# A decoder layer on one core: the 16 gated-attention units as seven block products, made ahead of the attention

## The chip, the core and the metric

The kernel runs on one core of one Trainium2 chip. A core has five engines that each follow their own list of instructions in order and wait for each other by semaphores: TensorE (PE, matrix products; its weight loads are shown apart, as PEld), VectorE (DVE), ScalarE (ACT), GpSimd (POOL) and SyncE (SP). In this kernel nearly every transfer between memory and the core is issued by SyncE, one after the other. The metric is the device time of one launch in microseconds, the median of several runs.

## The reference

One layer of a decoder, all in float32, for 1024 tokens and a model width of 2048:

```python
h = rmsnorm(x, g_pre)                       # over the 2048 columns
u = h @ w_in                                # split into the groups below
gq, gk, gv, g_gate, g_lr, sq, sk, sv, s_gate = split(u)
log_a = log_sigmoid(g_lr @ w_a2 + b_a) / 16
o_gla = gla_chunked(gq, gk, gv, log_a)      # 4 heads: q and k of 128 columns, v of 256
o_gla = rmsnorm(o_gla, g_gla_head) * silu(g_gate)
o_sb  = stick_breaking(sq, sk, sv) * silu(s_gate)   # 8 heads of 128 columns
mix = concat(o_gla, o_sb) @ w_out
x = x + rmsnorm(mix, g_post)
x = x + sigmoid(x @ w_ple_gate + b) * (p @ w_ple_proj)
```

The gated linear attention (GLA) keeps a state that decays by `log_a`; the stick-breaking attention weights position s for query t by `sigmoid(z_ts)` times the product of `1 - sigmoid(z_tj)` over the positions between them.

## The kernel before

Activations lie transposed: 128 features on the partitions, tokens along the free axis, in two halves of 512 tokens (`hf`). `x` is 16 blocks of 128 features. The columns of `w_in` that the attention needs are cut into 40 units of 128 columns: 16 for GLA (k, q and two of v for each of four heads), 24 for stick-breaking (k, q, v for each of eight heads).

Every float32 operand is split into two rounded parts, a high `hi` (ACT copies) and a low `lo` (VectorE subtracts), and a product is three matmuls: hi x hi, lo x hi, hi x lo. `split` (L111 to L113) does this everywhere, for weights and activations.

`dense` (L143) makes one unit: for each of 16 feature blocks and both halves three matmuls of 128x128 by 128x512 into a PSUM tile `dn`, 96 in all. Four weight quarters of 256 KB are loaded by `wload`, each into one of two `raw` buffers, and split into one of four `hi` and `lo` buffers. The norm of x is not applied to x: a unit's result is multiplied by `rstd` when it leaves PSUM. The first two units are interleaved with the loading of x, and the low-rank gate (`lr_ps`) with them.

After every feature block `dense` calls `step`, which lets other work move on: one piece of the queue `urgent`, and `rate[1]` pieces of the queue `jobs`. Jobs are generators: `gla(h)` for each GLA head and `sb()` for all stick-breaking heads. Each `yield` ends a piece. Thus the attention is laid between the dense products, by default in the order of the program; the scheduler may then move instructions by priorities (`high_priority` lifts weight loads and the emptying of PSUM) and by its own estimate of when operands are there. What it leaves on each engine is fixed when the kernel is built.

A stick-breaking head has 12 scores (6 items of two). For each score (`scores`): three matmuls into a PSUM tile `z` (two buffers), two sigmoids on ACT (into a tile `kq` with the tag X, L588, and a tile `sg` with the tag E or E2, L589), on diagonal blocks three GpSimd instructions, a reversed product scan on VectorE (L599), a multiply (L604), and `turn_by_dma` (L327): ACT copies the result apart into 16-bit planes in another X tile (L329), and a DMA transposes it into an E tile. X and E have two buffers each. The transposed weights are put together (L614) and split 8 pieces later, and multiplied with V another 8 pieces later. V itself is turned in the same way, by `turn`, through one X and one E tile for each half.

Before the change each unit's result goes straight into an SBUF tile of the attention (`evac_plain`, or `evac_turned` for V), so a head starts when its units are made, and a stick-breaking head waits for its three.

The later stages (the gate columns of `w_in`, `w_out`, `w_ple_gate`) already work by seven block products: the operands are cut into two by two blocks, sums S1 to S4 of blocks are kept in memory, and seven products of half the width replace eight, by Winograd's form of Strassen's scheme. The sums of x for the gates are made by `x_sums` beside the units.

Of the kernel before, what the change touches and what calls it, by code (L numbers as in the profile page):

```python
# [18 lines left out]
P = 128  # L19
# [26 lines left out]
RATE_GLA = 1.0  # L46
W0, W1, W2 = 3, 6, 1
RATE_SB = 0.9
# [5 lines left out]
LAG = 10  # L54
RATE_BG = 0.5
RATE_TAIL = 1.1
LAST_11 = 4
PACE_QKV, PACE_TAIL = 15, 4
# [3 lines left out]
def layer(ctx, tc, xT, w_in, w_gate, w_lr, w_a2, b_a, g_pre, g_head, w_out, g_post,  # L62
# [101 lines left out]
    pace = [0, PACE_QKV]  # L164
# [39 lines left out]

    def U(n):
        return [w_in[n, q] for q in range(4)]


    x_act = {hf: [None] * KT for hf in HALVES}
    pair = {}  # L210
    acc = {}
    lr_ps = {0: ps("t"), 1: ps("o")}
    first = [{hf: ps("dn") for hf in HALVES} for _ in range(2)]
    with tc.tile_pool(name="start", bufs=1) as sp:
        ones = sp.tile([P, P], F32, name="ones")
# [5 lines left out]
        lr_raw = sp.tile([P, KT, 16], F32, name="lr_raw")  # L221
        lr_w = sp.tile([P, KT, 32], F32, name="lr_w")
# [4 lines left out]
        raws = {hf: [] for hf in HALVES}  # L227
        squares_left = deque()

        def square(hf, k, raw):  # L230
            if k == 0:
                acc[hf] = new_rstd(hf)
                A.activation(acc[hf], raw, AF.Square)
                return
            sq = sp.tile([P, HT], F32, tag=f"sq{hf}", name=nm("sq"), bufs=2)
            A.activation(sq, raw, AF.Square)
            (V if hf == 0 else G).tensor_tensor(acc[hf], sq, acc[hf], op=ALU.add)

        for q in range(4):
            w = [wload(w_in[n, q]) for n in range(2)]  # L240
            for kk in range(4):
                k = 4 * q + kk
                sl = slice(kk * P, (kk + 1) * P)
                for hf in HALVES:
                    raw = sp.tile([P, HT], F32, tag="xraw", name=nm("xraw"), bufs=20)
                    dma(raw, part(xT[hf, k // 2], k))
                    raws[hf].append(raw)
                    if k % 2 == 0:
                        pair[hf] = act_wide(hf, k // 2)
                    ah, al = (part(t, k) for t in pair[hf])  # L250
                    x_act[hf][k] = (ah, al)
                    A.activation(ah, raw, AF.Copy, scale=gpre_s[:, k:k + 1])  # L252
# [15 lines left out]
        while squares_left:  # L268
            square(*squares_left.popleft())
# [475 lines left out]

# [613 lines left out]
```

## Time and profile before

| | us |
|---|---|
| median of 3 runs | 2095.12 (2091.56 to 2095.52) |
| the profiled execution | 2091.95 |
| its span, first to last instruction | 2089.9 |
| PE busy | 2068.4 (99%) |
| DVE busy | 1487.0 (71%) |
| ACT busy | 875.6 (42%) |
| POOL busy | 106.5 (5%) |

The profile names an instruction by its line, its engine, its operation and its tiles (out<-in, buffer numbers left out). Many instructions bear a helper's line: L101 is every matmul, L112 and L113 the two halves of every split. A wait row says which engine and line waited for which, the total in us, how often, and the longest. A window row gives a stretch of the span and its length, and then the busy time of PE, PEld, DVE, ACT and POOL, each with the number of instructions, the granted TensorE clock, the share of the DMA engines and GB/s. Matmuls overlap: the mean duration of one is longer than the time from one start to the next.

### The profile page before, as it was taken

To read this page: it belongs to the slowest core of one execution; us is meant where nothing else is said; L and a number is where in the kernel's file an instruction comes from. 1 tells how busy PE (TensorE), PEld (TensorE's weight loads), DVE (VectorE), ACT (ScalarE), POOL (GpSimd) and SP (SyncE) were. 2 spreads that over 40 slices of the span, in tenths; PEclk is the share of its full clock that TensorE was granted. 3 is DMA by queue.
4 is the path that set the end of the run, shared out by engine and by line. 5 is a ranking of instruction groups with operands and counts; after the bars stand their busy time and mean duration, and the time that the engine had idled before them with its cause. 6 is when DMAs were issued, how large, how long until landed. Compare 5 with 4: busy or idle time off the path is not lost.

```text
span 2089.9 us, 26754 instructions
## 1 busy us (share of the span) xinstructions
PE 2068.4 (99%) x9712; PEld 1708.3 (82%) x9712; DVE 1487.0 (71%) x2243; ACT 875.6 (42%) x1390; POOL 106.5 (5%) x228
## 2 busy tenths in 40 slices
PE   9999999999999999999999999999999999999998
PEld 6788888888888888888888788888888888787887
DVE  8657777676767667666567667788777787876665
ACT  7433333343455455555456413344233434323332
POOL 3100000000011011101001000000000000000000
PEclk9999999999999999999999999999999999999999
DMA  6222222222244344433336687888877586876663
GB/s 217 69 69 74 85 74 85 67 85 67 72 113 105 93 99 121 107 100 97 78 84 152 211 307 282 317 316 289 329 288 261 182 322 216 304 266 213 226 199 113
DMA packets 229812, 352.81 MB, mean 169 GB/s; under 512 B 124464, under 2 KB 129456, under 8 KB 229680
## 3 DMA queue, kind: packets, MB, share of 16 engines
q1 hardware_dynamic: 229104, 349.01, 52.1%
q10 hardware_dynamic: 576, 2.10, 0.3%
q8 instruction: 76, 1.25, 0.3%
q14 instruction: 56, 0.46, 0.1%
HBM read 249.85 MB, written 73.92 MB: 155 GB/s over the span
## 4 chain that ended last, share of the span: by engine, by line
PE 50%; DVE 9%; DMA 8%; issue 2%; ACT 2%; POOL 0%; SPq 0%; DVEq 0%; ACTq 0%; POOLq 0%
PE dn L101 45%; DMA wr<-w_g 3%; PE z L101 2%; PE t L101 2%; DVE wl L113 2%; DMA E<-X 2%; DMA wr<-w_out 1%; PE o L101 1%; DVE wr L872 1%; DVE al L113 1%; DMA ar<-og_d 1%; DVE ar L869 1%; DVE X L599 1%; DVE wr L869 1%; DVE ev L869 0%
## 5 line engine op out<-in xcount | busy, mean ns | idle before, releaser
L101 PE MATMUL dn<-ah,hi 128*128 128x512 f32 x1408 | 563.2, 400 | 1.5 <-ACT hi L112 1.3
L101 PE MATMUL dn<-al,hi 128*128 128x512 f32 x1408 | 551.0, 391 | 0.2 <-DVE al L253 0.2
L101 PE MATMUL dn<-ah,lo 128*128 128x512 f32 x1408 | 550.8, 391 | 0.2 <-DVE lo L113 0.2
L101 PE MATMUL dn<-ah,wl 128*128 128x512 f32 x1216 | 474.1, 390 | 2.2 <-DVE wl L113 2.2
L101 PE MATMUL dn<-al,wh 128*128 128x512 f32 x1216 | 473.7, 390 | 0.0
L101 PE MATMUL dn<-ah,wh 128*128 128x512 f32 x1216 | 473.7, 390 | 0.0
L101 PEld LDWEIGHTS dn<-ah,hi 128*128 128x128 f32 x1408 | 265.8, 189 | 60.7 <-ACT ah L252 3.4
L101 PEld LDWEIGHTS dn<-al,hi 128*128 128x128 f32 x1408 | 264.9, 188 | 58.1 <-DVE al L253 0.9
L101 PEld LDWEIGHTS dn<-ah,lo 128*128 128x128 f32 x1408 | 265.9, 189 | 48.2 <-DVE lo L113 0.5
L112 ACT ACTIVATE wh<-wr 128x1024 fp32r<-128x1024 f32 x152 | 158.9, 1056 | 307.5 <-DVE wr L872 150.1
L101 PEld LDWEIGHTS dn<-ah,wl 128*128 128x128 f32 x1216 | 228.4, 188 | 51.2 <-DVE wl L113 4.0
L101 PEld LDWEIGHTS dn<-ah,wh 128*128 128x128 f32 x1216 | 228.4, 188 | 47.6
L101 PEld LDWEIGHTS dn<-al,wh 128*128 128x128 f32 x1216 | 228.4, 188 | 47.0
L113 DVE TENSOR_TENSOR wl<-wr,wh 128x1024 fp32r<-128x1024 f32 x152 | 185.1, 1219 | 6.5 <-ACT wh L112 6.4
L112 ACT ACTIVATE hi<-raw 128x512 fp32r<-128x512 f32 x192 | 119.8, 626 | 147.3 <-PE dn L101 141.2
L113 DVE TENSOR_TENSOR lo<-raw,hi 128x512 fp32r<-128x512 f32 x192 | 134.7, 703 | 57.7 <-ACT hi L112 57.3
L329 ACT ACTIVATE X<-E 128x256 uint16<-128x256 uint16 (+2 forms) x96 | 81.0, 843 | 126.5 <-DVE E L604 118.9
L599 DVE TENSOR_TENSOR_SCAN X<-X 128x128 f32<-128x128 f32 (+2 forms) x96 | 98.3, 1024 | 30.9 <-POOL X L593 21.0
L872 DVE TENSOR_TENSOR wr<-wr,wr 128x1024 f32<-128x1024 f32 x48 | 58.7, 1224 | 76.4 <-issue 25.0
L614 DVE COPY v<-E 128x512 uint16<-128x512 uint16 (+1 forms) x160 | 63.6, 429 | 55.6 <-DMA E<-X 45.8
L869 DVE TENSOR_TENSOR wr<-wr,wr 128x1024 f32<-128x1024 f32 x48 | 58.8, 1224 | 46.9 <-DMA wr<-w_g 31.8
L113 DVE TENSOR_TENSOR s<-v,s 128x512 fp32r<-128x512 f32 (+1 forms) x82 | 52.3, 638 | 43.2 <-ACT s L112 39.6
(245 smaller groups left out, 2293.0 us busy)
## 6 DMA issues: line engine op xcount, KB each, us to landing
raw<-w_in SPq DMA_DIRECT2D x160, 256.0 KB, 2.7
wr<-w_g SPq DMA_DIRECT2D x64, 512.0 KB, 4.3
wr<-w_out SPq DMA_DIRECT2D x56, 512.0 KB, 4.8
wr<-w_gate SPq DMA_DIRECT2D x40, 512.0 KB, 5.2
g_d<-wr SPq DMA_DIRECT2D x32, 512.0 KB, 2.7
wr<-g_d SPq DMA_DIRECT2D x32, 512.0 KB, 4.9
ar<-h_d SPq DMA_DIRECT2D x28, 512.0 KB, 5.0
ar<-og_d SPq DMA_DIRECT2D x25, 512.0 KB, 4.8
```

What stands on the lines that cost most here:

```text
L101: PE.matmul(o, lhsT, rhs, start=start, stop=stop)
L112: A.activation(hi, src, AF.Copy)
L113: (eng or V).tensor_tensor(lo, src, f(hi), op=ALU.subtract)
L329: A.activation(pl.rearrange("p (two n) -> p two n", two=2), src.bitcast(U16)[:, :2 * n].rearrange("p (n two) -> p two n", two=2), AF.Copy)
L599: V.tensor_tensor_scan(rev, rev, rev, initial=kq[:, n:n + 1], op0=ALU.mult, op1=ALU.bypass)
L614: V.tensor_copy(to[:, :, :m, j], w[:, :, 2 * g:2 * g + m])
L869: V.tensor_tensor(dst, a, b, op=ALU.add)
L872: V.tensor_tensor(dst, a, b, op=ALU.subtract)
```

## The change

The 16 GLA units are made first, in a stage of their own ahead of all attention, with the same seven block products as the later stages: x in blocks A11 (first half of the tokens, first eight feature blocks), A12, A21, A22, and the weights in pairs of units (columns) by two halves of the features. Eight pairs `j` times seven products times eight feature blocks times three matmuls are 1344; by eight block products they were 1536.

- x is loaded several times, in pieces of 512 KB, and made into operands by `a12`, `sums`, `fill`, `again`. They advance by one piece for every second feature block (`PACE_E`). The sums S1 to S4 of x go to memory here, so `x_sums` is gone.
- Weights are loaded 512 KB at a time into four `wr` buffers, and split by halves into the same four `hi` and `lo` buffers. For five of the products they are sums of weight blocks; two of these are kept in memory.
- The results, not yet multiplied by `rstd`, go to memory (`un_d`). The 24 stick-breaking units are made by `dense` as before, and go to memory too, multiplied (`to_dram`).
- The attention loads everything back by new generators in `urgent`: `load_kq` and `load_v`, for GLA with the multiplication by `rstd`. The next GLA head's k and q are loaded towards the end of this head's first half, its V in the second half. A stick-breaking head's k and q are loaded at the fourth item of the head before; its V is loaded and turned when the head itself starts.
- All attention now lies beside the 24 stick-breaking units and the first gate products. `rate[1]` is 1.4 throughout (1.0, 0.9 and 1.1 before). Two of the gate products stand behind the attention's tiles, where four stood.

What this does to the order on two engines. First SyncE at the start of the program (raw and wr are weights, c the gains and other constants, lr_raw the low-rank weights, xraw and xr pieces of x). Before:

```order
1 L129 DMA raw_111<-w_in 128x512
2 L129 DMA raw_117<-w_in 128x512
3 L97 DMA c_75<-g_pre 128x16
4 L223 DMA lr_raw<-w_lr 128x256
5 L246 DMA xraw_123<-xT 128x512
6 L246 DMA xraw_135<-xT 128x512
7 L129 DMA raw_219<-w_in 128x512
8 L129 DMA raw_225<-w_in 128x512
9 L246 DMA xraw_147<-xT 128x512
```

And now:

```order
1 L441 DMA raw_167<-w_gla 128x512
2 L441 DMA raw_173<-w_gla 128x512
3 L259 DMA wr_290<-w_gla 128x1024
4 L259 DMA wr_340<-w_gla 128x1024
5 L441 DMA raw_223<-w_gla 128x512
6 L441 DMA raw_229<-w_gla 128x512
7 L259 DMA wr_382<-w_gla 128x1024
8 L259 DMA wr_428<-w_gla 128x1024
9 L95 DMA c_75<-g_pre 128x16
10 L240 DMA lr_raw<-w_lr 128x256
11 L451 DMA xr_181<-xT 128x512 x2
```

Eight weight loads stand ahead of the gains and of the first x, where two stood; the fifth takes a `raw` buffer that the first one's split must have read.

Second, ACT in the middle of a stick-breaking head. Before, behind the second score (X<-z and E<-z are the sigmoids, X<-E the plane copy, s and st splits for the products):

```order
585 L329 ACTIVATE X_6760<-E_1397_6748 128x512
586 L588 ACTIVATE X_6825<-z_6821 128x512
587 L112 ACTIVATE s_6799<-v_6796 128x384
588 L589 ACTIVATE E_6826<-z_6821 128x512
589 L112 ACTIVATE st_6932<-u_6010 128x128
590 L112 ACTIVATE hi_7068<-raw_7067 128x512
591 L329 ACTIVATE X_6832<-E_6826 128x1024
592 L588 ACTIVATE X_6846<-z_6842 128x512
```

And now, behind the second score of a head:

```order
784 L627 ACTIVATE X_9053<-E_1938_9043 128x512
785 L110 ACTIVATE hi_9586<-raw_9585 128x512
786 L627 ACTIVATE X_9078<-v_8973 128x1024
787 L110 ACTIVATE st_9213<-u_8732 128x128
788 L913 ACTIVATE X_9109<-z_9102 128x384
789 L110 ACTIVATE s_9016<-v_9013 128x512
790 L110 ACTIVATE s_9066<-v_9063 128x512
791 L110 ACTIVATE hi_9699<-raw_9698 128x512
792 L914 ACTIVATE E_9110<-z_9102 128x384
793 L110 ACTIVATE u_9076<-o_9136 128x512
794 L627 ACTIVATE X_9120<-E_9110 128x768
```

A plane copy of V (row 786) and the split of the turned V (row 793) now stand among the head's scores, and another pair behind the fourth score.

The diff, cut to its core:

```diff
-RATE_GLA = 1.0
-RATE_SB = 0.9
-RATE_TAIL = 1.1
-LAST_11 = 4
+RATE = 1.4
+E_GLA = 16
+LAST_11 = 2
+PACE_E, PACE_TAIL = 2, 4
...
+        def product(a, w):
+            p = ps("dn")
+            for k in range(8):
+                hi, lo = w[k // 4]
+                ...
+                mm(p, hi[:, sl], ah, k == 0, False)
+                mm(p, lo[:, sl], ah, False, False)
+                mm(p, hi[:, sl], al, False, k == 7)
+                estep()
+            return p
...
+        def fill(name, hf, kp0, make, wait=2):
+            pairs = []
+            for i in range(4):
+                raw, finish = make(i)
+                for _ in range(wait):
+                    yield 1
+                finish()
+                pairs.append(act_wide(hf, kp0 + i))
+                split(*pairs[-1], raw)
+                yield 1
+            sets[name] = parts(pairs)
...
+        for j in range(2, 8):
+            with ahead():
+                w = weight(wide_raw(w_gla[2 * j, 0]))
+            p = product(sets["A11"], w)
+            with soon():
+                A.activation(u(j), p, AF.Copy)
+        a = have("A12")
+        for j in range(8):
+            with ahead():
+                w = weight(wide_raw(w_gla[2 * j, 1]))
+            p = product(a, w)
+            with soon():
+                t = raw_tile()
+                add(t, p, u(j))
+                dma2(part(un_d[2 * j], 0), t)
+        s1, s2 = have("S1"), have("S2")
...
+        for j in range(8):
+            with ahead():
+                b11, t1, t2 = (wide_raw(w_gla[2 * j + n, kh]) for kh, n in ((0, 0), (0, 1), (1, 1)))
+                sub(t1, t1, b11)
+                sub(t2, t1, t2)
+                w2, w1 = weight(t2), weight(t1)
+                add(b11, b11, t2)
+                dma2(t2_d[j], t2)
+                dma2(t3_d[j], b11)
+            p = product(s2, w2)
+            with soon():
+                add(u(j), p, u(j))
+            p = product(s1, w1)
+            with soon():
+                add(v(j), p, u(j))
...
+        def to_dram(n):
+            t = keep.tile([P, W], F32, tag="ar", name=nm("ar"), bufs=3)
+            def go(hf, p):
+                V.tensor_tensor(part(t, hf), p, rstd[hf], op=ALU.mult)
+                if hf == 1:
+                    dma2(un_d[n], t)
+            return go
...
+        def load_v(todo, parts, scale):
+            def load(n, hf):
+                t = at("v")
+                dma2(t, part(un_d[n], hf))
+                return t
+            vt = load(*todo[0][:2])
+            for _ in range(3):
+                yield 1
+            for i, (n, hf, dst) in enumerate(todo):
+                if scale:
+                    V.tensor_tensor(vt, vt, rstd[hf], op=ALU.mult)
+                dst[hf] = at("u") if parts == 1 else (at("u", dt=F32R), at("u", dt=F32R))
+                t = turn(vt, dst[hf], parts)
+                next(t)
+                if i + 1 < len(todo):
+                    vt = load(*todo[i + 1][:2])
+                yield 1
+                yield from t
...
             for h in range(SB_HEADS):
-                while h not in sb_ready or (h == 0 and urgent):
+                kp, qp, vp = heads[GLA_HEADS + h]
+                while len(qp) < 2:
                     yield from pause(1)
-                kp, qp, vp = sb_ready.pop(h)
                 if h == 0:
                     to_sb()
+                urgent.append(load_sb_v(h))
...
                 for item in items:
                     hf, pr, c0 = item
+                    if item == items[3] and h + 1 < SB_HEADS:
+                        urgent.append(load_sb(h + 1))
                     rows = [scores(hf, 2 * pr, c0)]
...
+        rate[1] = RATE
+        urgent.extend((low_rank(0), low_rank(1), load_gla(0), load_gla_v(0)))
+        jobs.extend([gla(h) for h in range(GLA_HEADS)] + [sb()])
+        for n in range(E_GLA, 40):
+            dense(U(n), x_act, HALVES, to_dram(n))
+            if (n - E_GLA) % 3 == 2:
+                produced.add((n - E_GLA) // 3)
```

400 lines of the change are left out of this document (264 added, 136 removed).

## The prediction

> **What bounds the kernel now.** I read the page's busy line first, then TensorE's waits, then the windows of the stages that the change touches.
>
> ```profile
> PE 2068.4 (99%) x9712; PEld 1708.3 (82%) x9712; DVE 1487.0 (71%) x2243; ACT 875.6 (42%) x1390; POOL 106.5 (5%) x228
> ...
> PE t L101 <- ACT s L112: 2.5, 1, 2.5
> PE dn L101 <- DVE wl L113: 2.2, 2, 1.5
> ...
> 1205.00:1345.00 140.00, 140.00 (x618) 115.60 (x618) 98.74 (x98) 39.74 (x40) 0.00 (x0) 1.00 0.83 297
> ```
>
> TensorE has no free time, and its longest single wait is 2.5 us. In the pure product stretch (a window row gives the length, then PE, PEld, DVE, ACT and POOL busy with their counts, clock, DMA share and GB/s) 618 products take 140.00 us: **0.2265 us each**, from start to start. I use this spacing throughout, not the mean duration of one, since products overlap. So a removed product shortens the program, as long as what stands between the products keeps pace. That is the question here: the change squeezes the attention into fewer products.
>
> **What is removed.** Sixteen units by eight block products are 16x16x2x3 = 1536 matmuls; seven block products over 8 column pairs are 7x8x8x3 = 1344. So 192 fewer, 192 x 0.2265 = **-43.5 us**. The products of the other units, of the gates and of the attention are as many as before.
>
> **The start.** SyncE now issues eight weight loads (four of 256 KB, four of 512 KB, 3.1 MB) before the gains, the low-rank weights and the first piece of x; before, two of 256 KB stood there.
>
> ```profile
> 2.67 0.91 SPq L246 DMA_DIRECT2D xraw<-xT  x2
> 5.03 0.93 SPq L129 DMA_DIRECT2D raw<-w_in  x2
> 7.31 0.72 ACT L252 ACTIVATE ah<-xraw,c 128x512 fp32r<-128x512 f32 x1 [2.43 <-DMA xraw<-xT]
> 8.30 0.50 PE L101 MATMUL dn<-ah,hi 128*128 128x512 f32 x1
> 6.00:8.00 2.00, 0.93 (x5) 0.23 (x3) 0.42 (x1) 0.69 (x2) 0.00 (x0) 1.00 0.98 312
> 1162.00:1164.00 2.00, 0.89 (x3) 0.67 (x4) 0.74 (x2) 1.50 (x3) 0.00 (x0) 0.50 0.93 290
> 1164.00:1166.00 2.00, 2.00 (x7) 1.81 (x8) 1.78 (x4) 0.82 (x2) 0.00 (x0) 0.50 0.99 208
> 1166.00:1168.00 2.00, 2.00 (x6) 1.52 (x6) 1.31 (x4) 0.83 (x2) 0.00 (x0) 0.50 0.99 303
> ```
>
> The third piece of weights waits for a buffer that a split frees (5.03 us here), and x stands behind it. At 312 GB/s, 3.1 MB plus 0.4 MB of small constants and x need some 11 us from about 2 us on: x lands near 13.4, the first product follows 1 us later, at about 14 instead of 8.3, +6. The gap from the warm-up matmuls to there is longer than the one near 1160 us, after which the granted clock read 0.50 for 6 us, so I add 1.5: **+7.5** (bounds 4 and 11).
>
> **The rest of the early stage.** Here nothing of the attention runs; VectorE gets 48 more weight splits, 32 wide sums and some 30 wide additions and splits, all of kinds that the later block products already do.
>
> ```profile
> L113 DVE TENSOR_TENSOR lo<-raw,hi 128x512 fp32r<-128x512 f32 x192 | 134.7, 703 | 57.7 <-ACT hi L112 57.3
> L869 DVE TENSOR_TENSOR wr<-wr,wr 128x1024 f32<-128x1024 f32 x48 | 58.8, 1224 | 46.9 <-DMA wr<-w_g 31.8 <-DMA wr<-g_d 11.7 <-issue 2.7
> 1345.00:1395.00 50.00, 50.00 (x222) 41.45 (x221) 46.01 (x49) 22.48 (x22) 0.00 (x0) 1.00 0.89 321
> 1205.00:2050.00 845.00, 840.03 (x3691) 691.70 (x3691) 637.12 (x670) 298.29 (x326) 0.00 (x0) 1.00 0.77 269
> ```
>
> 48 x 0.703 + 32 x 1.224 = 73 us of it. Counted row by row in the changed order, this stage holds about 230 us of VectorE in 310 us of products. The row at 1345 us shows that TensorE loses nothing with VectorE at 46.01 of 50 in such a stage, so this work is covered by the products; in all such stages together (last row) TensorE was idle 5 of 845 us. **+2** (0 to 10, if the operand that is filled for the next eight products comes late).
>
> **The gated heads.** Their work moves under about 1130 products, where it had about 1520 (counted in the two orders). New are 32 rescalings of what comes back from memory and the loads.
>
> ```profile
> 100.00:540.00 440.00, 439.52 (x2262) 366.24 (x2261) 310.38 (x618) 166.79 (x284) 16.14 (x14) 1.00 0.26 75
> 100.00:540.00 440.00, 377.03 (x1544) 283.10 (x1543) 22.03 (x32) 0.00 (x0) 1.00 0.26 75
> DVE s L426 <- PE z L101: 19.0, 20, 1.9
> L668 DVE TENSOR_TENSOR u<-u,rstd 128x512 f32<-128x512 f32 x4 | 2.7, 688 | 0.1
> ```
>
> The second row is that of the dense products alone. Of VectorE's 310 us, their splits and evictions are 1544/96 x (4 x 0.703 + 2 x 0.69) = 67 and the sums of x some 24; 219 are the heads'. With 32 x 0.69 = 22 more and 49 for the splits of 1130 products, that makes 290 in some 360 us: 0.8, still under the 0.92 of the row at 1345 us, and VectorE waited for TensorE here, not the reverse. I take **+6** (0 to 30).
>
> **The stick-breaking heads.** This is where I expect the loss. Rows of the windows, of all instructions and of the dense products alone:
>
> ```profile
> 640.00:1100.00 460.00, 457.36 (x2222) 384.76 (x2221) 303.79 (x581) 235.96 (x465) 48.16 (x146) 1.00 0.39 99
> 640.00:1100.00 460.00, 395.43 (x1635) 300.81 (x1633) 24.15 (x36) 0.58 (x1) 1.00 0.39 99
> ```
>
> 1635 x 0.2265 = 370.3 of the 457.4 us, so the other 587 TensorE instructions cost 0.148 each. In the changed order seven heads (from the first score of one to that of the next) hold 1067 dense products and 649 others: 241.7 + 96.1 = 338 us, **48.2 us a head**, one head straight after the other.
>
> Can a head be done in 48 us? Its twelve scores are one chain: ACT's sigmoid into X, VectorE's scan, its multiply, ACT's plane copy into the other X, the transposing DMA; ACT issues the next sigmoid only behind the plane copy, and X has two buffers. One link, and the twelve sigmoids of four heads (first and last start):
>
> ```profile
> 822.75 0.58 ACT L588 ACTIVATE X<-z 128x512 f32<-128x512 f32 x1
> 823.36 1.28 DVE L599 TENSOR_TENSOR_SCAN X<-X 128x512 f32<-128x512 f32 x1 [1.23 <-ACT X L588]
> 824.75 0.69 DVE L604 TENSOR_TENSOR E<-E,X 128x512 f32<-128x512 f32 x1
> 825.47 1.06 ACT L329 ACTIVATE X<-E 128x1024 uint16<-128x1024 uint16 x1 [1.14 <-DVE E L604]
> L588 ACT ACTIVATE X<-z x12: 257/536/587, 568.8 to 632.8; 128x512 f32<-128x512 f32 x6, 128x128 f32<-128x128 f32 x2, 128x256 f32<-128x256 f32 x2, 128x384 f32<-128x384 f32 x2
> L588 ACT ACTIVATE X<-z x12: 268/535/588, 644.4 to 699.9; 128x512 f32<-128x512 f32 x6, 128x128 f32<-128x128 f32 x2, 128x256 f32<-128x256 f32 x2, 128x384 f32<-128x384 f32 x2
> L588 ACT ACTIVATE X<-z x12: 260/527/579, 725.2 to 772.2; 128x512 f32<-128x512 f32 x6, 128x128 f32<-128x128 f32 x2, 128x256 f32<-128x256 f32 x2, 128x384 f32<-128x384 f32 x2
> L588 ACT ACTIVATE X<-z x12: 254/537/587, 1096.9 to 1158.7; 128x512 f32<-128x512 f32 x6, 128x128 f32<-128x128 f32 x2, 128x256 f32<-128x256 f32 x2, 128x384 f32<-128x384 f32 x2
> ```
>
> A full link takes 825.47 + 1.06 - 822.75 = 3.8 us. The fastest head takes 47.0 us to its twelfth sigmoid, with the last link **50.8**; no V was turned among its scores. The others took 64.0, 55.5 and 61.8 for the same eleven steps; and heads came every 75 us (644.4 to 1096.9 is six of them), so there was room. In the changed order both turns of the head's V stand among its scores (behind the second and the fourth), in the same X buffers. What one costs:
>
> ```profile
> 740.09 0.26 ACT L588 ACTIVATE X<-z 128x128 f32<-128x128 f32 x1
> 742.48 0.38 ACT L588 ACTIVATE X<-z 128x256 f32<-128x256 f32 x1
> ...
> 938.41 0.28 ACT L588 ACTIVATE X<-z 128x128 f32<-128x128 f32 x1 [2.00 <-PE z L101]
> 942.24 1.04 ACT L329 ACTIVATE X<-v 128x1024 uint16<-128x1024 uint16 x1
> 945.82 0.39 ACT L588 ACTIVATE X<-z 128x256 f32<-128x256 f32 x1 [1.04 <-DMA E<-X]
> ```
>
> The step from a 128 score to a 256 score is 2.4 us without a turn and 7.4 with one: 5.0 at most; the sigmoid waits for a DMA to leave its buffer. Since part of those 5 is other work I take 3.1 for each turn, 50.8 + 2 x 3.1 = 57.0 us a head, 8.8 more than TensorE's 48.2. TensorE works in order and a late score stops the dense products behind it, so eight heads cost 70 us. The chain may lag once without harm, by what two score banks and the distance to the value products hold: the head at 568.8 had 192 products and 57 others between its first and last score, 43.5 + 8.4 = 52 us, took 64.0, and TensorE lost only 1.8 (50 - 48.24):
>
> ```profile
> 600.00:650.00 50.00, 48.24 (x235) 40.02 (x234) 35.19 (x66) 27.84 (x52) 3.16 (x13) 1.00 0.39 100
> ```
>
> So I take off 12: **+58**. Bounds: a chain of 50.8 with the turns hidden, 8 x 2.6 - 12 = 9; and 61.8 + 3.8 = 65.6 in every head, 8 x 17.4 - 12 = 127. My value lies between the fastest head and the slow ones because the fastest had no turn and VectorE is fuller now. What the old stage lost is replaced by this price, **-7**:
>
> ```profile
> 560.00:1165.00 605.00, 597.84 (x2887) 501.84 (x2886) 403.29 (x765) 322.20 (x631) 64.55 (x192) 1.00 0.41 106
> ```
>
> **The sum**, against the profiled execution (2091.95, span 2089.9): -43.5 + 7.5 + 2 + 6 + 58 - 7 = +23, so 2115. The median of the runs shown is 3.2 above that execution; I leave the forecast at **2115 us**, inside what the terms can tell. Its own range is 2097 to 2140.
>
> **Rivals.** *The chain keeps up* (0.30): transfers and turns fall into gaps, as at 725 us, and heads take 50.8. Then -43.5 + 7.5 + 2 + 6 + 9 - 7 = -26, 2066. It decides at 54 us a head: there 8 x 5.9 - 12 = 35 eats up what the other terms leave. For it: the link itself is short, and VectorE has a fifth of its time left. Against: no head shown took 48, and the fastest had no turn.
>
> *Given back exactly* (0.10): heads of 53.5 to 54.5 us, so that the waiting comes to some 35; 2091 to 2099. All that speaks for it is that gain and price are of one size.
>
> *The waits halve the clock* (0.14): if each head's waiting comes in one lump of about 3 us, TensorE runs at 0.50 for up to 6 us behind it, as from 1162 to 1168, and loses 3 us a head more: 2115 + 24 = 2139. For it is that row; against it, 8.8 us spread over twelve scores are under 1 us each. [...]
>
> *The change doesn't shorten the products* has no chance worth a number: the order holds 192 fewer.
>
> **Chances.** My forecast has 0.46. What the measurement can tell from no change is about 0.2%, 4 us: faster 0.31, same 0.10, slower 0.59 (the forecast, less its low edge, and the clock). The range 2058 to 2145 takes in most of both sides.
>
> **What would show it.** Right: the early stage ends near 325 us with no long waits; the first product starts at 13 to 15 us; between some 660 and 1100 us the busy share of TensorE falls, the waits name z and t, o behind ACT's s or E, and twelve sigmoids span 50 us or more in every head, with E<-X waits behind them. Wrong: heads every 48 us with TensorE at 1.00, which is the first rival; a loss in the early stage or the gated heads instead, which would mean that VectorE or the loads set the pace there and my 2 and 6 were mis-sized.

## The result and the profile after

The changed kernel takes 2169.91 us (median of four runs, 2166.19 to 2171.17); the kernel before took 2095.32 beside it. The ratio is **1.0356** (95% interval 1.0339 to 1.0374): 3.6% slower. Slower was right; 2115 us was far too low, and 2169.9 lies above the range's upper end, 2145.

The page of the changed kernel, busy line, then TensorE's waits (us in total, times, the longest):

```profile
PE 2077.0 (96%) x9520; PEld 1662.7 (77%) x9520; DVE 1592.6 (73%) x2399; ACT 930.3 (43%) x1466; POOL 110.8 (5%) x228
...
PE z L99 <- ACT E L914: 22.1, 30, 2.5
PE t L99 <- DVE s L111: 10.5, 26, 0.7
PE t L324 <- DMA xr<-xT: 10.0, 1, 10.0
PE o L99 <- ACT s L110: 7.3, 12, 1.2
PE t L99 <- ACT s L110: 6.0, 13, 0.7
PE t L810 <- DVE E L708: 5.6, 5, 1.6
```

There are 192 matmuls fewer, 9712 to 9520, as forecast; yet TensorE is busy no less and idle 92 us (2169.4 - 2077.0) where it was idle 21.5. A matmul that no other overlaps, as the last one ahead of a wait, is counted with its whole length, 0.39 us, and not with the 0.2265 from start to start; so the busy line does not tell how much is lost. I use the windows instead, and subtract what the matmuls in them need at the prediction's prices. First all instructions, then the dense products (tile dn) of the same stretches: the third block of the early stage, the gated heads, the stick-breaking heads.

```profile
123.00:172.00 49.00, 43.68 (x174) 34.02 (x174) 36.71 (x48) 12.03 (x19) 0.00 (x0) 0.93 0.88 302
400.00:775.00 375.00, 364.71 (x1918) 293.74 (x1918) 288.81 (x602) 146.96 (x263) 16.69 (x14) 1.00 0.29 87
775.00:1295.00 520.00, 465.60 (x2135) 352.51 (x2134) 382.59 (x736) 315.33 (x609) 71.21 (x192) 0.98 0.55 145
...
123.00:172.00 49.00, 43.68 (x174) 34.02 (x174) 6.15 (x9) 0.00 (x0) 0.93 0.88 302
400.00:775.00 375.00, 288.80 (x1145) 208.90 (x1145) 16.18 (x24) 0.00 (x0) 1.00 0.29 87
775.00:1295.00 520.00, 355.45 (x1365) 249.88 (x1364) 19.52 (x29) 4.69 (x8) 0.98 0.55 145
```

- Third block: 174 products need 39.4 of 49 us; 9.6 are lost (TensorE stood idle for 5.3 of them).
- Gated heads: before, 718 short matmuls took what 1544 products left of 440 us, 0.126 each. Here 1145 x 0.2265 + 773 x 0.126 = 356.7 of 375; 18.3 are lost. This rests on the 0.126 of the kernel before; TensorE stood idle for 10.3.
- Stick-breaking heads: 1365 x 0.2265 + 770 x 0.148 = 423.1 of 520; **96.9 are lost**, 54.4 of them as idle time. The first to the last score is 777 to 1260 us: 87.6 are lost there, 8.8 to 13.7 in each head, 11 in the mean. The other 9 are lost behind the last head.

At the start the first product stands at 17.73 us, 9.4 later than the 8.30 before:

```profile
9.05 7.01 SPq L451 DMA_DIRECT2D xr<-xT  x8
...
15.91 1.88 PE L324 MATMUL t<-xr,lr_w 128*32 128x512 f32 x2 [10.01 <-DMA xr<-xT]
...
17.73 0.80 PE L99 MATMUL dn<-ah,hi 128*128 128x512 f32 x1
```

From there to 21.23 us eight products take 3.50 us in place of 8 x 0.2265 = 1.81, since the granted clock was 0.50 from 15 to 20 us. These 1.7 us, for which the forecast had 1.5, are not in the 9.4.

| term | forecast | measured |
|---|---|---|
| 192 products fewer | -43.5 | -43.5 |
| the start | +7.5 | +9.4 |
| the rest of the early stage | +2 | +9.6 |
| the gated heads | +6 | +18.3 |
| the stick-breaking heads | +58 | +96.9 |
| what their old stage lost | -7 | -7 |
| sum | +23 | +83.7 |

The spans differ by 79.5 us (2169.4 - 2089.9); the table is within 4.2 of it. So no gain was missing: the products were saved. The four terms of waiting came to 134.2 where the forecast had 73.5.

The sigmoids of all eight heads, and of two of them (first and last start):

```profile
L913 ACT ACTIVATE X<-z x96: 257/537/601, 780.7 to 1257.0; 128x512 f32<-128x512 f32 x48, 128x128 f32<-128x128 f32 x16, 128x256 f32<-128x256 f32 x16, 128x384 f32<-128x384 f32 x16
...
L913 ACT ACTIVATE X<-z x12: 259/536/597, 900.2 to 953.2; 128x512 f32<-128x512 f32 x6, 128x128 f32<-128x128 f32 x2, 128x256 f32<-128x256 f32 x2, 128x384 f32<-128x384 f32 x2
L913 ACT ACTIVATE X<-z x12: 259/536/582, 957.5 to 1011.2; 128x512 f32<-128x512 f32 x6, 128x128 f32<-128x128 f32 x2, 128x256 f32<-128x256 f32 x2, 128x384 f32<-128x384 f32 x2
```

The eighth head's first sigmoid starts at 1197.3 us, so seven heads take (1197.3 - 780.7) / 7 = **59.5 us each**; the forecast had 57.0. Twelve sigmoids span 53.0 and 53.7 us here and 52.8 or more in every head, as "50 us or more" had said.

### The profile page after: what moved, and what is told of

It is laid out like the page before. It is cut to its first block, busy times and chain, and to the rows that moved or that the text cites. A ratio compares the mean times of both kernels' runs of the same rounds, so it can differ in the third digit from the quotient of the medians.

```text
span 2169.4 us, 26781 instructions
## 1 busy us (share of the span) xinstructions
PE 2077.0 (96%) x9520; PEld 1662.7 (77%) x9520; DVE 1592.6 (73%) x2399; ACT 930.3 (43%) x1466; POOL 110.8 (5%) x228
## 4 chain that ended last, share of the span: by engine, by line
PE 51%; DVE 18%; DMA 16%; ACT 7%; issue 5%; POOL 1%; SPq 1%; DVEq 0%; ACTq 0%; POOLq 0%
PE dn L99 44%; DMA E<-X 5%; PE z L99 4%; DVE X L924 3%; PE o L99 2%; DVE lo L111 2%; ACT X L627 1%; DVE E L929 1%; PE t L99 1%; DMA wr<-w_gla 1%; DMA wr<-w_gate 1%; DMA wr<-e_d 1%; ACT X L913 1%; DVE wr L210 1%; DVE wl L111 1%
## 5 line engine op out<-in xcount | busy, mean ns | idle before, releaser
L99 PE MATMUL dn<-ah,hi 128*128 128x512 f32 x1344 | 532.8, 396 | 3.8 <-ACT hi L110 3.7
L99 PE MATMUL dn<-ah,lo 128*128 128x512 f32 x1344 | 531.4, 395 | 1.6 <-DVE lo L111 1.6
L99 PE MATMUL dn<-al,hi 128*128 128x512 f32 x1344 | 531.1, 395 | 0.0
L99 PEld LDWEIGHTS dn<-ah,hi 128*128 128x128 f32 x1344 | 254.5, 189 | 61.1 <-ACT hi L110 7.9
L99 PEld LDWEIGHTS dn<-ah,lo 128*128 128x128 f32 x1344 | 254.6, 189 | 51.4 <-DVE lo L111 3.7
L213 DVE TENSOR_TENSOR wr<-wr,wr 128x1024 f32<-128x1024 f32 x64 | 78.3, 1223 | 91.3 <-DMA wr<-w_out 23.3
L110 ACT ACTIVATE hi<-wr 128x512 fp32r<-128x512 f32 x108 | 65.6, 625 | 130.6 <-PE dn L99 74.5
L210 DVE TENSOR_TENSOR wr<-wr,wr 128x1024 f32<-128x1024 f32 x64 | 78.3, 1224 | 52.9 <-DMA wr<-w_g 29.2
L111 DVE TENSOR_TENSOR lo<-raw,hi 128x512 fp32r<-128x512 f32 x132 | 90.7, 687 | 34.5 <-ACT hi L110 33.7
L110 ACT ACTIVATE hi<-raw 128x512 fp32r<-128x512 f32 x132 | 82.7, 627 | 73.0 <-PE dn L99 64.5
L627 ACT ACTIVATE X<-E 128x256 uint16<-128x256 uint16 (+2 forms) x96 | 80.9, 843 | 63.3 <-DVE E L929 59.8
L111 DVE TENSOR_TENSOR lo<-wr,hi 128x512 fp32r<-128x512 f32 x108 | 75.4, 709 | 18.4 <-ACT hi L110 18.1
```

Source lines behind the costliest of these rows:

```text
L99: PE.matmul(o, lhsT, rhs, start=start, stop=stop)
L110: A.activation(hi, src, AF.Copy)
L111: (eng or V).tensor_tensor(lo, src, f(hi), op=ALU.subtract)
L210: V.tensor_tensor(dst, a, b, op=ALU.add)
L213: V.tensor_tensor(dst, a, b, op=ALU.subtract)
L627: A.activation(pl.rearrange("p (two n) -> p two n", two=2), src.bitcast(U16)[:, :2 * n].rearrange("p (n two) -> p two n", two=2), AF.Copy)
```

## The experiments

In each, the ratio and its interval are against the kernel before, run beside it; medians are set against the 2169.9 of the changed kernel, which was not run again beside them. The kernel before, run each time, came out between 2093.3 and 2097.5 us, so gains of a few us are uncertain by as much. What a stretch loses is worked out as above.

### What makes a head long: V's turns?

One turn in the changed kernel, on ACT. The second sigmoid of a 384 score stands still until VectorE has emptied the tile E that V was turned into (L638):

```profile
906.48 1.04 ACT L627 ACTIVATE X<-v 128x1024 uint16<-128x1024 uint16 x1
...
908.97 0.49 ACT L913 ACTIVATE X<-z 128x384 f32<-128x384 f32 x1
...
915.21 0.49 ACT L914 ACTIVATE E<-z 128x384 f32<-128x384 f32 x1 [2.90 <-DVE o L638]
```

The first experiment leaves the turns out altogether:

```diff
 def turn(vt, dst, parts):
+    if parts == 2:
+        split(*dst, vt)
+        yield 1
+        return
     w = turn_by_dma(vt, HT, V_MID[parts - 1], V_END[parts - 1])
```

> The changed kernel without the turning of V in the stick-breaking heads: V is split as it comes back from memory, untransposed (so the values of these heads are not the reference's). Its loads, the rest of the head and all products stay. In the profile of the changed kernel a head takes 59.5 us (780.7 to 1197.3 us is seven). Theory A, the turns between the scores make the heads long: their two steps cost 8 to 12 us of each head, heads come every 48 to 52 us, where TensorE's own 48 take over; 8 x 8 to 8 x 10 less: 2090 to 2108 us. Theory B, the chain of the twelve scores is too long by itself (it took 50.8 us with the last link at best before, in emptier stages) and the turns stand in gaps: heads of 56 us or more, 2140 to 2165 us.

2146.13 us, ratio 1.0231 (1.0203 to 1.0260): 23.8 less. The time is theory B's, but the first three heads came after 49.1, 50.6 and 49.7 us, as A has it, and the later ones after 55.8 to 63.6. One of each kind, all instructions and then the dense products:

```profile
829.00:880.00 51.00, 45.63 (x216) 33.98 (x217) 40.27 (x84) 33.53 (x68) 9.62 (x24) 1.00 0.50 124
1043.00:1101.00 58.00, 53.38 (x262) 43.80 (x261) 42.48 (x85) 33.20 (x70) 9.99 (x24) 1.00 0.49 127
...
829.00:880.00 51.00, 30.98 (x118) 21.18 (x118) 1.37 (x2) 0.00 (x0) 1.00 0.50 124
1043.00:1101.00 58.00, 41.62 (x167) 30.13 (x165) 2.63 (x4) 0.00 (x0) 1.00 0.49 127
```

The early head shows what the chain of twelve scores takes by itself, 50 us, close to the 50.8 of the prediction: TensorE needs only 118 x 0.2265 + 98 x 0.148 = 41.2 there. In the later one TensorE needs 167 x 0.2265 + 95 x 0.148 = 51.9, and the chain, if it is as long as in the early heads, 50; yet the head takes neither 50 nor 52 but 58. It loses 6.1 us; the five heads from 929 us on lose 2.3 to 10.8.

Since ACT had waited for V's landing in that kernel, which might have hidden a gain, it was repeated with the split as late as the turn had been (three more pieces and one):

> The kernel that leaves out the turning of V, but with its split as many pieces behind the load as the turn was. Without that delay ACT waited 19.2 us for V to land, and the heads took 49.6, 50.6, 49.7, 55.8, 57.5, 57.9 and 63.6 us. Theory A (the turns, 59.5 - 50 us in every head, and those waits hid most of it): all heads 48 to 52 us, 2095 to 2120 us. Theory B or C (the later heads are slow for another reason, VectorE's order with the gates' work): 2138 to 2148 us.

2154.84 us (1.0275, 1.0245 to 1.0305). Theory A had 48 to 52 us in all heads: the fourth to the seventh head took 57.1, 57.6, 58.3 and 63.5 us, where they had taken 55.8, 57.5, 57.9 and 63.6 without the delay. So short heads did not come back. The edit did not remove ACT's waits for V's landing, though (20.6 us here, 19.2 before), so it tests less than was meant. The 2138 to 2148 of the other theories were missed too, by 7 us.

Two more edits gave V's turn a tile of its own, once for V as it lands, once for its transposed half:

```diff
-    t = at("v")
+    t = at("v0" if parts == 2 else "v")        # x2
-V_MID, V_END, VW = ("X", "X"), ("E", "E"), 3
+V_MID, V_END, VW = ("X", "X"), ("E", "v0"), 3  # x3
-SB_BUFS = {"E2": 2, "s2": 2}
+SB_BUFS = {"E2": 2, "s2": 2, "v0": 1}          # both
```

> The changed kernel with a tile of its own for V as it comes back from memory in the stick-breaking heads; before it shared the only tile v with the transposed weights. Theory A1, the tile v is what the turn holds up: VectorE waited 21.5 us in this stage to put weights into v until ACT had copied V out; 2.7 us a head, 2145 to 2152 us. Theory A2, the turn holds up E or X: within 5 us of the changed kernel, 2165 to 2170 us.

> The changed kernel with a tile of its own for the transposed half of V in the stick-breaking heads; before it took one of the two tiles E. Theory A2, the tile E is what the turn holds up: ACT's second sigmoid waited 23.6 us in 13 places until VectorE had emptied V's E; 2.9 us a head, 2143 to 2150 us. Theory A1 (the tile v): 2165 to 2170 us.

2170.34 us (1.0357, 1.0315 to 1.0399) and 2163.64 us (1.0315, 1.0285 to 1.0346). The tile v costs nothing that can be told, though VectorE waits 21.5 us for it in the changed kernel; the tile E costs some 6 us, of the 24 that ACT waits, and its interval still touches that of the changed kernel. Both theories had more. A wait that a profile names is not yet time that its removal gives back. With V's own tile v the heads did become shorter, (1175.8 - 775.5) / 7 = 57.2 us, but 1196 products lay beside the eight in place of 1260, and the loss stayed: 461 - 1196 x 0.2265 - 738 x 0.148 = 80.9, 10 in each. So a head's length alone does not set the price.

### ACT's order

Sigmoids ahead of the plane copy of the score before, with a third X:

```diff
 A.activation(sg[:, :n], z[:, :n], AF.Sigmoid, scale=scale)
-"X": 2
+"X": 3                    # its padding 64 columns, now 16
+while pend:
+    pend.pop()()          # plane copy and transposing DMA of the score before
...
-return turn_by_dma(sg, n, "X", tag), n
+pend.append(...)          # the same, behind the next score's sigmoids
```

> The changed kernel with ACT's two sigmoids of a score ahead of the plane copy of the score before it, and a third tile X for that (64 columns of padding cut to 16 to make room). Theory B, the order sigmoid, scan, multiply, plane copy, next sigmoid is what sets a head's 59.5 us: ACT waited 59.8 us in this stage for VectorE's multiply ahead of the plane copies; the chain loses some 0.8 us at each of 96 scores and heads come every 50 to 54 us, 2110 to 2135 us. Theory C, the loss comes from how unevenly the pieces of attention lie between the products, not from this order: TensorE still waits some 10 us a head, 2160 to 2172 us.

2137.78 us (1.0209, 1.0186 to 1.0233): 32.1 less, the largest gain of a single edit, just outside the band of theory B (2110 to 2135) and far from C. One early and one later head, all and dense:

```profile
826.00:876.00 50.00, 46.51 (x217) 34.16 (x217) 41.29 (x84) 34.95 (x69) 9.08 (x24) 1.00 0.61 142
986.00:1040.00 54.00, 53.31 (x270) 44.95 (x269) 44.84 (x89) 35.67 (x73) 8.68 (x24) 1.00 0.59 147
...
826.00:876.00 50.00, 31.49 (x121) 21.68 (x121) 1.36 (x2) 0.00 (x0) 1.00 0.61 142
986.00:1040.00 54.00, 42.41 (x171) 30.70 (x170) 2.57 (x4) 0.00 (x0) 1.00 0.59 147
```

The early head is again 50 us, with the turns in it, and loses 8.4; the later one loses only 0.6 (171 x 0.2265 + 99 x 0.148 = 53.4). It is the best of the eight: the others lose 3.1 to 10.1. So the order on ACT and the third X together are part of the cause; the third X alone was not run, so they can't be told apart. Why 121 products lie in one head and 171 in another was not tested either; the scheduler places them.

### VectorE's load

The low half of the unit weights left out on VectorE, the high half multiplied in its place:

```diff
-    split(hi[:, :n], lo[:, :n], raw[:, :n], ...)
-return hi, lo
+    A.activation(hi[:, :n], raw[:, :n], AF.Copy)
+return hi, hi
```

> The changed kernel without VectorE's low half of the unit weights and of the first gate weights (TensorE multiplies the high half in its place, so the products of the low halves are not the reference's). TensorE, ACT and the loads have the same work; VectorE has some 0.69 us less for every 24 products, 33 us less under the gated heads (288.8 busy of 375) and 4.3 us less in a stick-breaking head (43 busy of 58). Theory D, VectorE is so full that everything that goes through it in order comes late: the waiting falls by as much, 15 us of the gated heads' 28 and 30 or more of the others' 101, 2115 to 2130 us. Theory B, ACT's order and the shared tiles make the chain: less than 10 us, 2160 to 2170 us.

2160.35 us (1.0306, 1.0287 to 1.0324), 9.5 less, just inside theory B's "less than 10". Theory D falls. The gated heads show it best; all and dense:

```profile
400.00:750.00 350.00, 339.07 (x1784) 271.67 (x1782) 256.51 (x547) 140.50 (x250) 15.60 (x14) 1.00 0.29 87
...
400.00:750.00 350.00, 265.93 (x1047) 191.00 (x1045) 14.96 (x22) 0.00 (x0) 1.00 0.29 87
```

VectorE's share goes from 0.77 to 0.73, and the loss from 18.3 to 350 - 1047 x 0.2265 - 737 x 0.126 = 20.0: nothing won there. Where the 9.5 us came from was not settled.

### How closely the attention lies

```diff
-RATE = 1.4
+RATE = 1.6       # x7
+RATE = 1.35      # x8
-LAST_11 = 2
+LAST_11 = 0      # x8
```

> The changed kernel with 1.6 pieces of attention for each feature block in place of 1.4, so that each head lies under an eighth fewer products and as many more follow behind. If the attention's own length decides (theories A and B), the eight heads and the four gated heads stay as long as they are and the products that no longer lie under them come on top: about 150 x 0.2265 / 8 = 4.2 us for each of eight heads and 80 x 0.2265 x 4 / 8 = 9 us or less for the gated ones, some 30 to 45 us more, 2200 to 2215 us. If the loss is of fixed size and place (buffers, drains), within 10 us of 2170.

> The changed kernel with 1.35 pieces for each feature block and all eight of the second gate products beside the attention in place of six. If the attention's own length decides, 48 more matmuls lie under it, 10.9 us less: 2156 to 2162 us. If the loss is of fixed size, 2167 to 2172 us.

2169.02 us (1.0353, 1.0327 to 1.0380) and 2183.26 us (1.0422, 1.0400 to 1.0445). The first is no test: in its trace a head still has 145 dense products of 242 matmuls, the changed kernel's 145 of 244. The number of pieces a block moves the program's order; here the scheduler's order hardly followed. The second was slower, against both theories. Seven heads took 427 us in it and 417 in the changed kernel; 19 more products lie beside them (4.3 us), and 6 us more are lost. One wait at the stage's end grew too, a gate weight behind ACT, from 4.5 to 11.8 us. Why was not settled.

So the distance had to be changed in another way: four of the eight stick-breaking heads are left out (their output is their k), which leaves products enough to lay the others apart.

```diff
+if h % 2:
+    for hf in HALVES:
+        dma2(part(o_d[hf][4 + h // 2], h), kp[hf])
+    ...
+    continue
-RATE = 1.4      # x12: as it was
+RATE = 1.0      # x13
```

> The changed kernel with only the even four of the stick-breaking heads computed (the others' outputs are filled with their k), laid as closely as before: 147 products from one head to the next by the order, 285 to 300 for a gated head. Both theories: four heads lose 10 to 12 us each, the gated heads 28 us together; less TensorE work of some 100 short matmuls in each head left out, 4 x 13 us: 2169.9 - 52 - 46 = 2072 us (2060 to 2085).

> The same four heads with 1.0 pieces for each feature block in place of 1.4: 234 products from one head to the next in place of 147, 372 for a gated head in place of 300. Theory E, the waiting comes from laying the attention closer than its chains of three engines run: the heads lose under 3 us each and the gated heads under 12 us together, so 4 x 8 + 16 = 48 us less than its twin, about 2025 us. Theory F, the waiting is of fixed size in each head (places where TensorE's order and the chain's do not fit): the same as its twin within 10 us.

2065.21 us (0.9870, 0.9851 to 0.9888) and 2046.93 us (0.9779, 0.9764 to 0.9795). One head of each; the close one, all and dense, then the one apart:

```profile
831.00:891.00 60.00, 53.34 (x252) 40.09 (x251) 44.69 (x88) 36.55 (x75) 9.29 (x24) 1.00 0.58 156
831.00:891.00 60.00, 39.39 (x152) 26.81 (x150) 2.63 (x4) 0.00 (x0) 1.00 0.58 156
```

```profile
908.00:979.00 71.00, 71.00 (x351) 60.16 (x350) 46.06 (x91) 36.54 (x74) 9.06 (x24) 1.00 0.54 148
908.00:979.00 71.00, 60.71 (x252) 45.98 (x251) 3.91 (x6) 0.00 (x0) 1.00 0.54 148
```

Close: 152 x 0.2265 + 100 x 0.148 = 49.2 of 60 us, **10.8 lost**. Apart: 252 x 0.2265 + 99 x 0.148 = 71.7 of 71, **nothing lost**. VectorE and ACT have the same work in both (44.7 and 46.1, 36.6 and 36.5 us); the products between differ. ACT's order is not quite the same: in the close head V's first plane copy stands ahead of the third score's sigmoids and its second ahead of the fifth's, in the one apart both stand ahead of the third's. That can't be what wins the whole 11 us: without any turn (the first experiment) heads still lost 2.3 to 10.8, 7 in the mean.

All four heads, worked out in the same way (start of the stretch: dense products, its length and what it loses, both in us):

| | close | apart |
|---|---|---|
| first head | 775: 152, 56, 10.9 | 842: 225, 66, 4.4 |
| second | 831: 152, 60, 10.8 | 908: 252, 71, none |
| third | 891: 158, 59, 9.6 | 979: 249, 74, 2.1 |
| fourth | 995: 181, 55, 3.3 | 1053: 206, 68, 8.9 |

The third close head has 45 us of plain products behind it, so the fourth is not quite close. In the first three pairs the same work loses 10 us a head under some 50 us of TensorE's work and 2 under 62 to 72. That is theory E, and it shows the main cause: the head is laid too close. The fourth pair does not follow it.

The twins differ by 18.3 us, though, not by the 48 of theory E, and not by the 10 or less of theory F. The last head apart and the drain behind it took back a part:

```profile
1053.00:1165.00 112.00, 95.93 (x413) 76.47 (x412) 72.84 (x127) 55.23 (x105) 8.05 (x23) 0.92 0.68 200
1053.00:1165.00 112.00, 80.61 (x305) 60.02 (x304) 6.17 (x9) 2.91 (x5) 0.92 0.68 200
```

305 x 0.2265 + 108 x 0.148 = 85.1 of 112: 27 lost, 17.8 of them from 1121 us on, behind the head's scores, where 100 products lie in 44 us. And the gated heads, by the order 186 products apart for each half in place of about 150, still lose 13.0 (418 - 1386 x 0.2265 - 723 x 0.126) where the close twin loses 16.3 (361 - 1115 x 0.2265 - 731 x 0.126). The rows of the one apart, all and dense:

```profile
407.00:825.00 418.00, 409.49 (x2109) 338.04 (x2108) 295.39 (x605) 149.88 (x260) 14.74 (x13) 0.99 0.29 88
407.00:825.00 418.00, 343.83 (x1386) 254.57 (x1385) 20.53 (x30) 0.00 (x0) 0.99 0.29 88
```

For them closeness explains about a fifth. What costs the gated heads their 18 us stays open; taking VectorE's share from 0.77 to 0.73 did not lower it. The largest wait of TensorE there, t behind VectorE's E (5.6 us, in the list of the changed kernel), was not followed up.

### The early stage

First weights, gains, low-rank weights and the first pieces of x ahead of the wide loads on SyncE, by priorities:

```diff
-with ahead():                                   # first pair's weights
+with tc.high_priority(offset=1500):
...
-    with ahead():                               # j = 2 to 5
+    with (ahead() if j > 5 else tc.high_priority(offset=40 * j - 70)):
         w = weight(wide_raw(w_gla[2 * j, 0]))
```

> The changed kernel with the first weights, the gains, the low-rank weights and the first pieces of x ahead of the wide weight loads on SyncE. The start term by the forecast: the first product moves from 17.7 us back to 9 to 10 us, 7 to 9 us less, 2161 to 2163 us. The rival: the wide weights then come late for the third pair, the stall moves there, and less than 3 us is won.

2160.67 us (1.0300, 1.0265 to 1.0335), 9.2 less, with the first product even earlier than 9 to 10 us:

```profile
7.21 0.50 PE L99 MATMUL dn<-ah,hi 128*128 128x512 f32 x1
```

The start term is confirmed in mechanism, and in size within its bounds (4 to 11). In the third block, two edits:

```diff
 sub(t1, t1, b11)            # x15: these three sums left out
 sub(t2, t1, t2)             # x15
 w2, w1 = weight(t2), weight(t1)
 add(b11, b11, t2)           # x15
-dma2(t2_d[j], t2)           # x14: both stores left out
-dma2(t3_d[j], b11)          # x14; later loads of t2_d and t3_d read w_gla
```

> The changed kernel without the two stores of summed weights in the third block of the early stage (16 of 512 KB); the later products load weights from w_gla in their place, so that the gated units are not the reference's. Sums and products stay. If the tiles wr that the stores hold are what makes the next weights late, the 9.4 us between 123 and 172 us fall to 2 or less: 2160 to 2164 us. If the sums are, less than 3 us: 2167 to 2170 us.

> The changed kernel without the three wide sums of weights for each pair in that block (24 of 1.22 us on VectorE; the gated units are not the reference's). Loads, stores and products stay. If the sums are what makes the weights late: 2160 to 2164 us; if the held tiles are: 2167 to 2170 us.

2167.02 us (1.0321, 1.0295 to 1.0348) and 2161.01 us (1.0304, 1.0283 to 1.0326). The stretch of the 9.6 us, without stores and without sums:

```profile
123.00:172.00 49.00, 47.62 (x208) 38.39 (x207) 38.22 (x48) 13.65 (x21) 0.00 (x0) 1.00 0.72 245
```

```profile
123.00:172.00 49.00, 49.00 (x218) 40.59 (x217) 25.13 (x37) 14.89 (x24) 0.00 (x0) 1.00 0.92 331
```

208 products need 47.1, 1.9 lost; 218 need 49.4, nothing lost. Either edit takes nearly all the waiting away, so it is one chain: load, two wide sums, splits, a third sum and two stores, in four tiles wr, for every 10.9 us of products. Without sums the whole time follows, 8.9 us. Without stores 2.9 us of the 7.7 won here arrive by the medians, 7 by the ratios to the kernel before, and the interval overlaps that of the changed kernel; so its expectations are not decided by the whole time, only by this stretch.

### Mended together

```diff
 # both: x5's sigmoids and third X, x4's order at the start
-"u": 12
+"u": 11
+V_END = ("E", "v1")   # x10: V's transposed half in its own tile
+"st": 3               # x11: in its place a third tile of the split query
```

> The changed kernel with three edits together: sigmoids ahead of the plane copies with a third X (alone 2137.8), the start's order (alone 2160.7) and V's transposed half in a tile of its own (alone 2163.6); 11 tiles u in place of 12 make the room. If the gains add up, 2169.9 - 32.1 - 9.2 - 6.3 = 2122 us. If the second and third answer to the same wait (E and X held too long), 2127 to 2130 us. If the tile u that is taken away makes the loads of the next head late, over 2135 us.

> Sigmoids ahead of the plane copies, the start's order, 11 tiles u, and a third tile st for the split query in place of V's own tile. ACT waited 20.4 us in 28 places for TensorE to free st, and behind ACT the whole chain. If those waits are on the chain, 2.5 us a head less than the sum of the two edits of 2128 us: 2105 to 2115 us. If they only fill time in which ACT had nothing to do, 2125 to 2132 us.

2128.48 us (1.0149, 1.0127 to 1.0171) and 2123.69 us (1.0125, 1.0097 to 1.0153). The first is 41.4 less than the changed kernel, where the single gains sum to 47.6. V's own tile and the third X may answer in part to the same waits, or the tile u that was taken away may cost; the 6 us are too few to tell. The third tile st gives no more than V's own tile did: against the 2128 worked out for the two other edits some 5 us, where 13 to 23 were expected if those waits were on the chain. It tests little: with the sigmoids ahead, ACT's waits for st had already fallen from 20.4 to 4.1 us, and the third tile brought them to 2.0. The best kernel that computes everything is so still 1.25% slower than the one before.

## Why the prediction was right and wrong

**Right.** The removed products are worth their 43.5 us, all of it. The loss sits where it was put: in the stick-breaking heads, with the waits named there (z behind ACT's E, t and o behind s), and in SyncE's order at the start. The head's chain without turns, 50.8, is 48 to 51 from one early head to the next in both kernels without turns. The head as it stands, 57.0, is 59.5; that this came so near is luck, as the paragraph on the turns shows. Two signs were missed: the first product came at 17.73 us, not at 13 to 15, and the early stage did have a long wait.

**The step that failed** is "+58", the step from the head's length to its price, with the 12 taken off for lag. It took a head as the longer of two things, the chain of 57.0 or TensorE's 48.2 us: 8 x 8.8 - 12. Measured in the changed kernel, the heads lose 87.6, 11 each where 8.8 stood, which is 18 more; the 12 for lag were not earned; and 9 are lost in the drain behind the last head, which had no term. 58 + 18 + 12 + 9 = 97, the 96.9 measured. That the longer of the two is not the right rule, the kernel without turns shows: where TensorE needs 51.9 and the chain, by the early heads, 50, a head takes 58. Its eight heads lose 60.5 together (780 to 1215 us: 435 - 1175 x 0.2265 - 732 x 0.148), where the rule, with a chain of 50.8 and the 46.8 that TensorE needs for one there, gives 8 x 4.0 = 32. So the price begins before the chain is clearly the longer one, and it all but goes in three of the four heads laid apart.

What makes up the price within a head stays open. A first guess is that the two wait for each other. In the changed kernel from 780 to 1260 us ACT, and what stands behind it in order, waits in 39 places for TensorE to free a tile, 32.4 us:

```profile
ACT X L627 <- DVE E L929: 59.8, 75, 2.5
...
ACT st L110 <- PE z L99: 20.4, 28, 1.3
ACT hi L110 <- PE dn L99: 12.0, 11, 3.0
```

But these waits are at most a part of the price. In the first kernel without turns they are 5.0 us in all, and its heads lose the 60.5; with the sigmoids ahead they are 9.9, and the heads lose 55.1 (437 - 1200 x 0.2265 - 744 x 0.148). In the late head without turns shown above TensorE itself waits 4.6 us in six places, 3.1 of it for ACT's second sigmoid to free z: single scores come late although the whole chain, by the early heads, is no longer than its cover.

The lag bought nothing: already the first head loses what the others lose, 57.00 - 153 x 0.2265 - 72 x 0.148 = 11.7:

```profile
777.00:834.00 57.00, 51.26 (x225) 39.92 (x225) 41.16 (x80) 34.58 (x67) 10.31 (x24) 0.94 0.47 119
777.00:834.00 57.00, 40.58 (x153) 29.20 (x153) 1.35 (x2) 0.00 (x0) 0.94 0.47 119
```

The old head at 568.8, from which the credit was taken, had 75 us to itself; the experiment with heads apart fits with room, not lag, having made it cheap.

**Turns.** "3.1 for each turn", 16 of them, are 50 us; without them 23.8 were won, or 15.1 in the repeat. This term was too large, by 26 to 35 us, and the price of nearness had no term. The two errors made the 57.0 come out almost right.

**"The gated heads +6"** were judged by VectorE's share, 0.8 against the 0.92 of a stage of mere products. That gauge failed: with VectorE at 0.77 the stage loses 18.3 us, and at 0.73 no less, while the stage of products lost nothing at 0.92. There the splits run ahead of the products; in the heads VectorE is one link of a chain over three engines. That this is the reason is argued, not shown. The 18.3 lies inside the bounds given (0 to 30).

**"The rest of the early stage +2"** covered VectorE's work by the products, from the same gauge; what came late was a chain of loads, sums and stores. 9.6 lies in its bounds too (0 to 10). All four terms came short, each inside its own bounds, and the range was too narrow for that: at the upper bounds of the four terms the sum is -43.5 + 11 + 10 + 30 + 127 - 7 = +127.5, 2219, and the range stopped at 2145.

**The rivals.** "The chain keeps up" did not happen. "Given back exactly" neither. "The waits halve the clock" is a small part: the row of the first head above has 0.94, the second 0.97, the third 1.00. By the stage's mean, 0.98 of 520 us, it is an estimated 10 us at most of the 96.9, with the drain. The lump of 3 us in each head did not come either; TensorE's longest wait for a score is 2.5 us.

```profile
834.00:897.00 63.00, 54.99 (x251) 41.21 (x250) 43.40 (x87) 36.42 (x72) 9.47 (x24) 0.97 0.50 121
897.00:955.00 58.00, 52.94 (x251) 39.99 (x250) 44.07 (x85) 36.91 (x74) 9.18 (x24) 1.00 0.48 125
```

## What to carry to other kernels

Work that is laid beside products was only hidden here while its own chain was clearly shorter than TensorE's work above it: the same head, with a chain of 50 to 57 us, cost 0 to 2 us under 72 us of TensorE's work, 4 to 9 under some 60 and 11 under 49. So before saving products, count for each stage how many remain as cover for each chain, and price a chain of about the same length as its cover at more than the difference. An engine's busy share said little of this here; lay the work apart in an experiment, and see whether the waiting goes.

## What was not expected of the hardware

The forecast's "+2" for the rest of the early stage has no part for a lower clock. In the third block TensorE stood still for 2.89 us, and the granted clock was 0.51 from 161 to 168 us, for longer than the wait itself:

```profile
158.66 0.39 PE L99 MATMUL dn<-al,hi 128*128 128x512 f32 x1
161.94 0.80 PE L99 MATMUL dn<-ah,hi 128*128 128x512 f32 x1 [2.89 <-ACT hi L110]
...
161.00:164.00 3.00, 1.74 (x3) 1.12 (x4) 2.97 (x5) 2.19 (x4) 0.00 (x0) 0.51 1.00 411
164.00:168.00 4.00, 4.00 (x11) 3.06 (x10) 2.73 (x5) 0.00 (x0) 0.00 (x0) 0.51 0.67 235
168.00:170.00 2.00, 2.00 (x11) 1.62 (x10) 1.14 (x1) 0.00 (x0) 0.00 (x0) 1.00 0.62 229
```

Of the 9.6 us lost there some 2.9 are the clock's: from 161.94 to 167.91 us 12 products took 5.65 us (0.32 of waiting taken off), and 12 x 0.2265 is 2.7. The kernel before had the same; the clock of 0.50 from 1162 to 1168 us, which the prediction shows, begins within a wait of 2.54 us:

```profile
1163.11 1.95 PE L101 MATMUL t<-s,u 128*128 128x256 f32 x6 [2.54 <-ACT s L112]
```
